# Adaptive max pooling in one dimension: which engine's DMA queue carries the loads and stores

## The chip, the core and the metric

The kernel runs on one core of one Trainium2 chip. The time is device microseconds of one execution; three executions of the kernel before took 335.21, 335.26 and 334.77 us, so the median is 335.21 us. A separate execution was taken with the hardware profiler; its span, from the first to the last instruction, is 333.1 us.

Five engines have instruction streams: PE (TensorE), DVE (VectorE), ACT (ScalarE), POOL (GpSimd) and SP (SyncE). In this kernel only DVE computes. SP and ACT issue DMA transfers. "SPq" and "ACTq" in the profile are the instruction sequencers of SyncE and ScalarE, "q1" and "q10" the DMA queues that the two fill. 16 DMA engines move the bytes of both queues.

## The reference

```
x = randn(32, 256, 4096), float32
output_size = 256
for i in range(output_size):
    start = int(i * length / output_size)
    end = int((i + 1) * length / output_size)
    result[:, :, i] = np.max(x[:, :, start:end], axis=-1)
```

4096 is 256 times 16, so every output is the maximum of its own 16 neighbouring inputs. 134.2 MB are read and 8.4 MB written.

## The kernel before

The input is seen as one long list of windows of W = 16 values, the output as the list of their maxima. There are 2,097,152 windows, or 16,384 for each of the 128 partitions. A "column" is one window in all 128 partitions. A load brings n columns; VectorE reduces them by `reduce_max` over the innermost 16 values (the helper `pooled`, line 56); the maxima of all but the last load stay in SBUF in the tile `kept`.

The 16,384 columns are cut into two groups. Group A has ten loads: FIRST = 128 columns (1,024 KB), eight loads of CHUNK = 1024 columns (8,192 KB each), and one of 1020 columns (8,160 KB). Group B has six loads of 1024 columns and a last one of 900 columns (7,200 KB). Within a group, one partition's windows lie next to each other in memory, so that one partition's share of a load is one contiguous run (64 KB for a load of 1024 columns), and the maxima of a whole group can be stored with one contiguous run for each partition.

The loads go into one tile, `ring`, of 2352 columns. The short first load goes to columns 1024 to 1151 (line 87). The 16 other loads (line 96) alternate between the lower and the upper half, and each half is shifted by GAP = 152 columns every second time. A load may overwrite its place in the ring once VectorE has read what lay there. Because of the shift, the next load into a half needs only the larger part of the chunk before it to be reduced: each chunk is reduced in two instructions, the part that the next load needs first (872 columns), the rest (152 columns) second. So the load with number n + 2 waits for the larger reduction of chunk n, and no longer.

In this text the short first load is called the first load, the 16 others are load 0 to load 15. Load 0 and load 1 wait for nothing; load 2 waits for VectorE's larger reduction of load 0, and also for the landings of the first load and of load 0.

VectorE's instructions run in order: first the first load's reduction (128 columns), then two for each of the loads 0 to 14, then one for load 15, whose 900 maxima are written back into the ring (`last_kept`).

There are three stores: the last store (line 114, 450 KB: the 900 maxima of load 15), and two large ones from `kept` (line 117): store 1 with group A's maxima (4,670 KB) and store 2 with the rest of group B (3,072 KB). `tc.no_sync_barrier()` stands between line 114 and line 117 in the program text. Since each engine runs its own stream, in order, the stores that one engine issues start behind the loads that the same engine issues. In the kernel before, SyncE's stream is: first load, loads 0 to 15, store 1, store 2, then the waits at the end of the program for every transfer (line 148). ScalarE's stream has a single transfer, the last store.

Each waiting transfer waits on its engine's sequencer: an instruction that waits holds up all that is behind it in the same stream.

Of the kernel before, what the change touches and what calls it, by code (L numbers as in the profile page):

```python
# [1 line left out]

# [4 lines left out]


@with_exitstack
def kernel(  # L10
    ctx: ExitStack,
    tc: tile.TileContext,
    x: bass.AP,
    output_size: bass.AP,
    out: bass.AP,
):

    nc = tc.nc
    P = nc.NUM_PARTITIONS
    fp32 = mybir.dt.float32

    B, C, L = x.shape
    O = int(output_size)  # L30
    assert L % O == 0, (L, O)
    W = L // O
    total = B * C * O // P
    assert B * C * O % P == 0

    CHUNK = 1024
    GAP = 152
    FIRST = 128
    LOADS_A, LOADS_B = 9, 6

    LESS = 4
    group_a = [FIRST] + [CHUNK] * (LOADS_A - 1) + [CHUNK - LESS]
    last = total - sum(group_a) - LOADS_B * CHUNK
    group_b = [CHUNK] * LOADS_B + [last]
    assert 0 < last and last * (W + 1) <= CHUNK * W

    pool = ctx.enter_context(tc.tile_pool(name="pool", bufs=1))
    ring = pool.tile([P, 2 * (CHUNK + GAP) * W], fp32, tag="ring", name="ring")
    kept = pool.tile([P, total - last], fp32, tag="kept", name="kept")

    xw = x.flatten_outer_dims().rearrange("r (o w) -> (r o) w", w=W)
    ow = out.flatten_outer_dims().rearrange("r o -> (r o)")

    def pooled(dst, at, n):

        nc.vector.reduce_max(  # L56
            out=dst,
            in_=ring[:, at * W : (at + n) * W].rearrange("p (n w) -> p n w", w=W),
            axis=mybir.AxisListType.X,
        )  # L60

    taken = 0

    def group(n):

        nonlocal taken
        span = slice(taken * P, (taken + n) * P)
        taken += n
        return (
            xw[span].rearrange("(p n) w -> p (n w)", p=P),  # L70
            ow[span].rearrange("(p n) -> p n", p=P),
        )

    stores = []
    n_loads = 0
    base = 0
    for g, loads in enumerate((group_a, group_b)):
        xg, og = group(sum(loads))
        a = sum(loads) if g == 0 else 0
        for n in loads:  # L80
            if g == 0:
                a -= n
            xn = xg[:, a * W : (a + n) * W]
            dst = kept[:, base + a : base + a + n] if n != last else None
            if n == FIRST:

                nc.sync.dma_start(  # L87
                    out=ring[:, CHUNK * W : (CHUNK + n) * W], in_=xn
                )
                pooled(dst, CHUNK, n)  # L90
            else:

                low = n_loads % 2 * (CHUNK + GAP)
                moved = n_loads // 2 % 2
                at = low + moved * GAP
                nc.sync.dma_start(out=ring[:, at * W : (at + n) * W], in_=xn)
                if n != last:
                    cut = CHUNK - GAP if moved else GAP
                    parts = [(0, cut), (cut, n)]
                    for u, v in parts if moved else parts[::-1]:  # L100
                        pooled(dst[:, u:v], at + u, v - u)
                else:
                    end = (at + CHUNK) * W
                    last_kept = ring[:, end - n : end]
                    pooled(last_kept, at, n)
                n_loads += 1
            if g:
                a += n
        full = a - last if g else sum(loads)
        stores.append((og[:, 0:full], kept[:, base : base + full]))  # L110
        base += full
    assert taken == total

    nc.scalar.dma_start(out=og[:, full : full + last], in_=last_kept)
    tc.no_sync_barrier()
    for dst, src in stores:
        nc.sync.dma_start(out=dst, in_=src)


# [1 line left out]
_INS = ['x', 'output_size']  # L121
_OUTS = [((32, 256, 256), 'float32')]

_NUMBERS = {'output_size': 256}


# [26 lines left out]
```

## Time and profile before

| What | us |
|---|---|
| Median of 3 runs | 335.21 |
| Span of the profiled execution | 333.1 |
| VectorE busy (32 instructions) | 276.5 |
| Reduction of 872 columns, mean of 14 | 14.69 |
| Reduction of 152 columns, mean of 15 | 2.68 |
| Reduction of the last 900 columns | 15.14 |
| Reduction of the first 128 columns | 2.29 |
| From one chunk's first reduction to the next one's | 19.35 |
| VectorE idle before each chunk | 2.07 |

The profile gives busy time for engines, the times at which DMA transfers were issued, and the times at which they landed, that is, when their semaphore had its full count. "SPq <- DVE" in a table of waits means that SyncE's sequencer stood at an instruction until VectorE's work released it. The DMA share of a stretch of time is the mean share in which the 16 DMA engines were busy; the rate in GB/s counts all bytes that they moved.

### The profile page before, as it was taken

To read this page: it belongs to the slowest core of one execution; us is meant where nothing else is said; L and a number is where in the kernel's file an instruction comes from. 1 tells how busy PE (TensorE), PEld (TensorE's weight loads), DVE (VectorE), ACT (ScalarE), POOL (GpSimd) and SP (SyncE) were. 2 spreads that over 40 slices of the span, in tenths; PEclk is the share of its full clock that TensorE was granted. 3 is DMA by queue.
4 is the path that set the end of the run, shared out by engine and by line. 5 is a ranking of instruction groups with operands and counts; after the bars stand their busy time and mean duration, and the time that the engine had idled before them with its cause. 6 is when DMAs were issued, how large, how long until landed. Compare 5 with 4: busy or idle time off the path is not lost.

```text
span 333.1 us, 113 instructions
## 1 busy us (share of the span) xinstructions
DVE 276.5 (83%) x32; POOL 0.2 (0%) x4
## 2 busy tenths in 40 slices
DVE  2009979797997979799797979979797998979993
POOL 0000000000000000000000000000000000000000
DMA  9898989899898989899898989899898989899997
GB/s 378 378 504 378 504 378 504 378 449 433 378 504 378 504 378 504 378 441 441 384 494 377 504 378 504 378 456 425 386 496 378 504 378 504 378 458 443 393 395 330
DMA packets 2880, 142.61 MB, mean 428 GB/s; under 512 B 320, under 2 KB 320, under 8 KB 448
## 3 DMA queue, kind: packets, MB, share of 16 engines
q1 hardware_dynamic: 2736, 142.15, 98.8%
q10 hardware_dynamic: 144, 0.46, 0.3%
HBM read 134.22 MB, written 8.39 MB: 428 GB/s over the span
## 4 chain that ended last, share of the span: by engine, by line
DMA 57%; DVE 36%; DVEq 5%; issue 0%; SPq 0%
DMA ring<-in_x_dram 57%; DVE kept L56 36%; DVEq L148 5%; SPq L87 0%
## 5 line engine op out<-in xcount | busy, mean ns | idle before, releaser
L56 DVE TENSOR_REDUCE kept<-ring 128x152 f32<-128x2432 f32 (+3 forms) x31 | 261.4, 8473 | 51.5 <-DMA ring<-in_x_dram 51.5
L56 DVE TENSOR_REDUCE ring<-ring 128x900 f32<-128x14400 f32 x1 | 15.1, 15143 | 0.0
L134 POOL MEMSET const-bfloat16-1.0<- 128x1 bf16 x1 | 0.1, 103 | 0.0
L134 POOL MEMSET const-uint8-127<- 128x1 uint8 x1 | 0.1, 102 | 0.0
L134 POOL MEMSET const-float32-0.0<- 128x1 f32 x1 | 0.1, 100 | 0.2 <-issue 0.2
L134 POOL MEMSET const-float32-1.0<- 128x1 f32 x1 | 0.1, 99 | 0.0
## 6 DMA issues: line engine op xcount, KB each, us to landing
ring<-in_x_dram SPq DMA_DIRECT2D x1, 8160.0 KB, 23.9
ring<-in_x_dram SPq DMA_DIRECT2D x1, 7200.0 KB, 21.7
out_dram<-kept SPq DMA_DIRECT2D x1, 4670.0 KB, 32.4
out_dram<-kept SPq DMA_DIRECT2D x1, 3072.0 KB, 18.2
ring<-in_x_dram SPq DMA_DIRECT2D x1, 1024.0 KB, 4.7
out_dram<-ring ACTq DMA_DIRECT2D x1, 450.0 KB, 4.2
ring<-in_x_dram SPq DMA_DIRECT2D x14, 24.0
```

The lines of the kernel that those rows point to most:

```text
L56: nc.vector.reduce_max(out=dst, in_=ring[:, at * W : (at + n) * W].rearrange("p (n w) -> p n w", w=W), axis=mybir.AxisListType.X,)
L134: nc = _bacc.Bacc("TRN2", target_bir_lowering=False, num_devices=1)
L148: with _tile.TileContext(nc) as tc:
```

## The change

Three words in the program change. The 16 loads of line 96 and the two large stores of line 117 are issued from ScalarE instead of SyncE; the last store of line 114 is issued from SyncE instead of ScalarE. The first load stays on SyncE.

```
-                nc.sync.dma_start(out=ring[:, at * W : (at + n) * W], in_=xn)
+                nc.scalar.dma_start(out=ring[:, at * W : (at + n) * W], in_=xn)
...
-    nc.scalar.dma_start(out=og[:, full : full + last], in_=last_kept)
+    nc.sync.dma_start(out=og[:, full : full + last], in_=last_kept)
     tc.no_sync_barrier()
     for dst, src in stores:
-        nc.sync.dma_start(out=dst, in_=src)
+        nc.scalar.dma_start(out=dst, in_=src)
```

ScalarE's stream is then: loads 0 to 15, store 1, store 2, each with the waits that it had on SyncE. SyncE's stream is: first load, last store, and the waits at the end of the program. The streams of VectorE, GpSimd and TensorE hold the same instructions in the same order. The first load and load 0, which had followed each other on one queue, are on two queues.

## The prediction

> **What bounds the kernel now.** I read the DMA line of the page and a table of stretches first, because 83% busy on VectorE leaves open who waits for whom.
>
> ```profile
> span 333.1 us, 113 instructions
> DVE 276.5 (83%) x32; POOL 0.2 (0%) x4
> ...
> q1 hardware_dynamic: 2736, 142.15, 98.8%
> q10 hardware_dynamic: 144, 0.46, 0.3%
> ```
>
> ```profile
> core 0: us, DVE busy (x) POOL busy (x), PEclk, DMA share, GB/s
> 0.00:1.70 1.70, 0.00 (x0) 0.20 (x4) 1.00 0.00 0
> 1.70:312.60 310.90, 261.11 (x31) 0.00 (x0) 1.00 1.00 434
> 312.60:331.80 19.20, 15.36 (x2) 0.00 (x0) 1.00 0.95 406
> 331.80:333.10 1.30, 0.00 (x0) 0.00 (x0) 1.00 0.00 0
> ```
>
> The two queues' packets fill 99.1% of 16 engines' span. From 1.7 us to the last load's landing the engines are busy all the time, at 434 GB/s; only 1.7 us at the start and 1.3 us at the end hold no packets, and the last 19 us run a little under the rate. So the bytes set the time: 142.61 MB / 434 GB/s = 328.6 us of 333.1. A change of queue can win or lose only at the start, at the end, or where it lets the engines run dry.
>
> Next, how far the engines are from running dry: SyncE's waits, and the order of time around load 2.
>
> ```profile
> SPq L96 <- DVE kept L56: 205.5, 14, 14.7
> SPq L96 <- DMA ring<-in_x_dram: 78.4, 14, 22.7
> SPq L117 <- DVE kept L56: 21.1, 1, 21.1
> ```
>
> ```profile
> 24.78 17.28 DVE L56 TENSOR_REDUCE kept<-ring 128x872 f32<-128x13952 f32 x2 [17.05 <-DMA ring<-in_x_dram]
> 39.49 0.33 SPq L96 DMA_DIRECT2D ring<-in_x_dram  x1
> 44.13 14.69 DVE L56 TENSOR_REDUCE kept<-ring 128x872 f32<-128x13952 f32 x1 [2.07 <-DMA ring<-in_x_dram]
> ```
>
> Fourteen loads are issued the moment VectorE ends an 872-column reduction. Load 2 goes out at 39.49, while load 1 lands at 44.13: the engines have 4.64 us of work left. VectorE idles 2.07 us before each chunk, so a delay of VectorE shrinks by 2.07 us with every chunk.
>
> The issue table gives the latency and the end:
>
> ```profile
> out_dram<-kept SPq DMA_DIRECT2D x1, 4670.0 KB, 32.4
> out_dram<-kept SPq DMA_DIRECT2D x1, 3072.0 KB, 18.2
> ring<-in_x_dram SPq DMA_DIRECT2D x1, 1024.0 KB, 4.7
> out_dram<-ring ACTq DMA_DIRECT2D x1, 450.0 KB, 4.2
> ```
>
> On SyncE the first load, issued at 0.73, lands 4.7 us later; 1.049 MB at 434 GB/s are 2.4, so the lead from issue to steady flow is 2.3 us. On ScalarE the only row is the last store: 4.2 − 0.461 MB / 434 GB/s = 4.2 − 1.1 = 3.1 us, part of which is time behind store 2. I take 2.3 for ScalarE too, the row of the same kind of transfer on idle engines, and keep 3.1 as the upper bound and 2.3 as the lower, since nothing in the trace suggests a shorter one.
>
> **The change part by part.**
>
> *Sixteen loads to ScalarE.* An issue took 0.33 to 0.43 us on SyncE (median 0.33 of 16) and 0.37 on ScalarE: sixteen by +0.04 are 0.6 us of sequencer time. Fourteen lie inside the 4.64 us of work left; with a lead of 2.3 us 2.3 are spare, with 3.1 still 1.5. On the path: 0. Without that cover each issue would cost 0.04 us. The wait list of each load is the same (VectorE and earlier landings), and nothing else runs on ScalarE, so what queues behind a waiting load is again only the next load and the stores.
>
> *Store 1 and store 2 to ScalarE.* They follow load 15 in one stream, as before: store 1 is issued at 291.37 and flows behind the last load (landed 312.64); store 2, which waits 21.1 us for VectorE, goes out at 312.93 and flows behind store 1 (landed 291.37 + 32.4 = 323.8). It has 10.9 us of cover against 2.3 to 3.1. Sum: 0. With no cover the 2.3 to 3.1 would show in full.
>
> *The last store to SyncE.* SyncE's stream holds only the first load ahead of it and the final waits behind it; those waits end with the landings anyway. VectorE ends at 327.96, the issue follows at 327.99. Store 2 lands at 312.93 + 18.2 = 331.1, the last store at 332.2, 1.1 us later, which is just its bytes. So its lead lies beside store 2: with 2.3 us it is ready at 330.3, 0.8 before store 2 is through. Without that cover 2.3 us would show. An issue of 0.33 to 0.43 instead of 0.37 is −0.04 to +0.06 inside those 0.8 us: 0.
>
> *The start.* Load 0 was issued second on SyncE, at 1.16; now ScalarE issues it at once. Released at 0.649 (SyncE) and 0.653 (ScalarE) in the trace, the two begin within 0.01 us of each other, so load 0 and load 1 reach the engines together with the first load. In all, the bytes are the same, so the flow ends at the same time if it begins at the same time. What can change is when it begins (below), and which load comes first. If an engine serves load 0 first, the first load lands not at 5.4 but as late as both loads' bytes, 24.76. VectorE's order is fixed, so it starts with the 128 columns then: 24.78 + 2.29 + 14.69 = 41.76, load 2 goes out at 41.78 instead of 39.49. 44.13 − 41.78 = 2.35 are left against a lead of 2.3: still nothing lost, by 0.05 us. VectorE's 152 columns end at 44.44, 0.3 late for load 1, gone in the next 2.07 of idle time. With the lead of 3.1 it costs 0.8. So this part is 0 to +0.8, and I take 0.
>
> The sum is 0: span 333.1. Outside the span lie 335.2 − 333.1 = 2.1 us, which I keep: 335.2 us, the median of the runs shown (334.77 to 335.26).
>
> **A rule to weigh here.** In the trace each transfer has 144 packets (2736 are 19 transfers, 144 one), nine for each engine. On every engine the last store's packets begin only after store 2's last one, at 330.2 and later, though it was issued at 327.99. Either a begun transfer is finished before another queue gets the engine, or a queue keeps the engine until it is empty; store 2 was the last on its queue, so the trace can't tell. The Trainium skill ("DMA: Bandwidth & Descriptors", section "Queues, rings and completion order") says that an engine takes turns between the queues that have work and changes over after a whole packet of, typically, 9 to 17 descriptors. By that rule the first load waits for load 0 at most and the sum stays 335.2 to 336.0; by the harsher reading of the row it is the third rival's 354.5.
>
> **The rivals.**
>
> *A faster start.* Load 0's issue moves from 1.16 to 0.73, 0.43 us earlier, and two queues are filled at once. First load and load 0 together are 9.44 MB, 21.7 us at 434 GB/s, and landed at 24.76: in effect the flow began at 3.0. The first packet is at 1.75, and a landing comes 0.4 after its packets, so 3.0 − 1.75 − 0.4 = 0.9 us is the most to be had. For it: the first packets took 0.3 to 1.1 us where later ones of their size took 0.31. Against it: no packet can come before the first issue at 0.73, which stays. 334.8 by the issue alone, 334.3 at most.
>
> *Load 2 comes late.* The first load falls behind load 0, and ScalarE's lead is over 2.35 us: then the engines run dry at 43 to 44 us, once. From 2.35 on each microsecond of lead costs one; at 3.1 it is 0.8: 336.0. For it: the dead heat at the start. Against it: the 3.1 contains time behind store 2.
>
> *The first load falls behind load 0 and load 1.* If a queue keeps the engine until it is empty, and ScalarE's is first on even one engine, the first load lands at 44.13. VectorE, which needs it first, then ends load 0's larger part at 44.15 + 2.29 + 14.69 = 61.13; load 2 flows from 61.13 + 2.3 = 63.4 instead of 44.1. That is 19.3 us of empty engines, which nothing later gives back: 354.5. For it: the row above allows it. Against it: SyncE is released first, and it needs both conditions; half for the first and a quarter for the second are 0.12.
>
> That the change does nothing at all is the forecast's own neighbour and gives the same 335.2.
>
> **How the numbers follow.** A difference under 0.2% (0.67 us) can't be told from none here. Forecast, no part on the path: 0.56, of which 0.48 within 0.67 us, 0.04 faster and 0.04 slower by what the runs scatter. Faster start: 0.15, of which 0.08 over 0.67 us. Load 2 late: 0.17, of which 0.10 over 0.67. Behind both loads: 0.12, all slower. Faster 0.04 + 0.08 = 0.12; slower 0.04 + 0.10 + 0.12 = 0.26; same 0.62. Predicted time 335.2. The range goes from 334.3, the faster start's end, to 336.0, load 2 late at the upper lead; the 354.5 and some scatter stay outside.
>
> **What would show it.** Right: the DMA rate stays 434 GB/s from 1.7 us to the last load's landing, the span is 333.1 within 0.7, and VectorE idles 2.07 us before each chunk from load 2 on. First load behind load 0: VectorE's first reduction starts at 20 to 25 us instead of 5.4. Load 2 late: a hole in the DMA share near 43 us. Behind both loads: VectorE idle until 44. Faster start: load 0 lands before 24.7 with all else shifted alike. Wrong in the whole: a DMA rate other than 434 GB/s on ScalarE's queue, which no row of a large load there can exclude.

## The result and the profile after

The changed kernel took 337.62 us in the median of six executions (335.52, 337.45, 337.62, 337.62, 337.66, 337.66), the kernel before 335.09 us beside it. The ratio is 1.0065, with a 95% interval of 1.0052 to 1.0078: it is slower, and outside the range of 334.3 to 336.0 us. The executions form two groups, one at 335.5 and five at 337.5 to 337.7; the profile on record for the changed kernel is of the execution at 335.52 us.

From its page, the span, the queues and the issues (KB, us from issue to landing):

```profile
span 333.7 us, 113 instructions
...
q10 hardware_dynamic: 2592, 141.10, 97.8%
q1 hardware_dynamic: 288, 1.51, 1.3%
...
out_dram<-kept ACTq DMA_DIRECT2D x1, 4670.0 KB, 32.4
out_dram<-kept ACTq DMA_DIRECT2D x1, 3072.0 KB, 18.1
ring<-in_x_dram SPq DMA_DIRECT2D x1, 1024.0 KB, 22.3
out_dram<-ring SPq DMA_DIRECT2D x1, 450.0 KB, 4.2
```

The bytes have changed queues, and the stores land as fast as before (32.4, 18.2 and 4.2 us then). One row is different: the first load takes 22.3 us to land, where it took 4.7. The order of time shows what hangs on it:

```profile
0.72 39.79 ACTq L96 DMA_DIRECT2D ring<-in_x_dram  x3
0.72 0.37 SPq L87 DMA_DIRECT2D ring<-in_x_dram  x1
23.04 19.70 DVE L56 TENSOR_REDUCE kept<-ring 128x128 f32<-128x2048 f32 x3 [23.04 <-DMA ring<-in_x_dram]
44.82 14.69 DVE L56 TENSOR_REDUCE kept<-ring 128x872 f32<-128x13952 f32 x1 [2.08 <-DMA ring<-in_x_dram]
```

VectorE's first reduction starts at 23.04 instead of 5.4, and load 1 is there at 44.82 instead of 44.13, 0.7 late. That is this execution's whole loss. A later profile of the same kernel (the last experiment below) was of an execution at 337.48 us, and its chain of waits, start and length of each piece, shows the rest:

```profile
span 335.7 us, 113 instructions
```

```profile
0.73 24.72 DMA ring<-in_x_dram
25.45 0.02 issue
25.47 16.89 DVE kept L56 x2
42.36 0.02 issue
42.39 23.55 DMA ring<-in_x_dram
65.94 0.02 issue
65.96 14.70 DVE kept L56
```

Now the first load lands at 25.45. VectorE needs 16.89 us for it and for load 0's larger part, load 2 goes out at 42.39 instead of 39.49, and lands at 65.94 instead of 63.45: 2.5 us late. Everything after that runs at the old pace, some 2.5 us later.

The single packets show how the two loads share the engines. Their rows, put together from the trace's packet records (us; for each load the range over the 16 engines; the records do not name the engine, so packets that follow one another without a gap are taken as one engine's):

```
                        before       changed,     changed,
                                     335.52 us    337.48 us
load 0, last ends       23.96-24.40  23.99-25.08  24.04-25.07
load 1, last ends       43.28-43.73  43.31-44.40  43.37-44.40
load 2, first starts    43.28-43.73  43.31-44.40  43.70-45.39
load 2, last ends       62.60-63.08  62.76-63.72  63.73-65.58
last packet of all      331.72       332.37       334.34
```

On each engine a packet of the first load (8 KB) and one of load 0 (64 KB, 2.42 us) take turns, one by one. Eight such turns put the end of the first load beside the end of load 0. In the execution at 335.52 us two packets of the first load came ahead of load 0's first on every engine, so its ninth packet, the 4 bytes that count the landing, went in front of load 0's eighth. In the one at 337.48 us only one came ahead, and that ninth packet had to wait behind load 0's eighth: 2.42 us, within 0.01 the difference between 23.04 and 25.47. The loss of 2.5 us then has two parts in the table, read on the slowest engine: 0.67 at the start (25.07 against 24.40) and 1.83 where load 2 arrives (65.58 − 63.08 − 0.67). Ten of the 16 engines ran dry, for up to 2.0 us. The engine that ended load 2 last was through with load 1 at 43.55, got load 2's first packet at 45.36 and took 3.30 us for it instead of 2.42.

### The profile page after: what moved, and what is told of

It is laid out like the page before. It is cut to its first block, busy times and chain, and to the rows that moved or that the text cites. A ratio compares the mean times of both kernels' runs of the same rounds, so it can differ in the third digit from the quotient of the medians.

```text
span 333.7 us, 113 instructions
## 1 busy us (share of the span) xinstructions
DVE 276.5 (83%) x32; POOL 0.2 (0%) x4
## 4 chain that ended last, share of the span: by engine, by line
DMA 58%; DVE 36%; DVEq 5%; issue 0%
DMA ring<-in_x_dram 58%; DVE kept L56 36%; DVEq L148 5%
## 6 DMA issues: line engine op xcount, KB each, us to landing
out_dram<-kept ACTq DMA_DIRECT2D x1, 4670.0 KB, 32.4
ring<-in_x_dram SPq DMA_DIRECT2D x1, 1024.0 KB, 22.3
```

## The experiments

The executions of the kernel before that ran beside these had medians of 334.93 to 335.03 us. "Order theory" and "queue theory" are explained in the first expectation below.

**The changed kernel again.** No edit.

> The changed kernel again. Of its six executions one took 335.5 us (the profiled one) and five 337.5 to 337.7. Order theory: ScalarE's load 0 and SyncE's first load start in a dead heat; where load 0's packets come first on the engines, the first load's last packets fall behind packets of load 1 (2.4 us each), it lands at 26 to 27 us, VectorE comes late to load 0, load 2 goes out at about 44 instead of 40 us, and the engines run dry for about 2 us. It expects two groups of times again, near 335.5 and near 337.6, and nothing between. Queue theory: ScalarE's queue is itself slower, by a slower start of some engines or a lower rate; it expects times that spread evenly from 335.5 upward, and load 2 issued near 40 us in every profile.

Measured: 335.72 once, the profiled one, and 337.08 to 337.83 five times; ratio 1.0065 (1.0049 to 1.0081). The profile has the first load at 23.26 and load 2 at 40.40. Two groups and nothing between, as the order theory has it, but the profile shows only the group that loses little.

**VectorE's order.** The first load goes to a place that load 2 does not need, and is reduced behind load 0's larger part:

```
-                    out=ring[:, CHUNK * W : (CHUNK + n) * W], in_=xn
+                    out=ring[:, 2200 * W : (2200 + n) * W], in_=xn
...
-                pooled(dst, CHUNK, n)
+                late = (dst, 2200, n)
...
                         pooled(dst[:, u:v], at + u, v - u)
+                        if late is not None:
+                            tc.no_sync_barrier()
+                            pooled(*late)
+                            late = None
```

> The changed kernel, but the first load goes to columns 2200 to 2327 (which load 3 and not load 2 overwrites) and VectorE reduces it after load 0's 872 columns, so nothing on the way to load 2 waits for the first load. The two loads still race at the start. Order theory: all executions at 335.0 to 335.8 us, whichever load comes first, VectorE's first reduction at 24.4 to 25.5 and load 2 issued 14.7 us later, at 39 to 40.3. Queue theory: the loss does not depend on VectorE's order, so most executions stay at 337 to 338 us.

Measured: 335.45 to 335.72 us in eleven executions, ratio 1.0016 (1.0007 to 1.0025). The chain of waits:

```profile
0.72 25.07 DMA ring<-in_x_dram
25.80 0.02 issue
25.82 14.70 DVE kept L56
40.52 0.02 issue
40.54 23.80 DMA ring<-in_x_dram
```

In the profiled execution only one packet of the first load came ahead on every engine, as in the one at 337.48 us, and it still took 335.71 us. The upper group is gone, so its 1.9 us pass through VectorE's wait for the first load. What remains, 0.6 us, is the start itself: load 0 is there at 25.82 instead of 24.78. VectorE's order has no part in that.

**SyncE held back.** One line ahead of the first load:

```
+                nc.vector.memset(ring[:, CHUNK * W : CHUNK * W + 64], 0.0)
```

> The changed kernel, but the first load waits for a memset of 64 values per partition in its place by VectorE, so that SyncE issues it 0.1 to 0.4 us after ScalarE's load 0. Order theory: load 0's packets come first on all engines; the first load lands at 24.4 to 27 us, load 2 goes out at 41.5 to 44.2, and all executions are in the upper group, 337 to 338.5 us, the profiled one too, with a hole in the DMA work near 44 us. Queue theory: the small delay of a load that is not the bound changes nothing: the same mixture as the changed kernel, load 2 near 40 us.

Measured: 336.75 to 337.78 us in five executions, ratio 1.0068 (1.0056 to 1.0080). SyncE issued 0.23 us behind ScalarE, and load 0's packets came first on all engines:

```profile
25.44 16.89 DVE kept L56 x2
42.33 0.02 issue
42.35 23.57 DMA ring<-in_x_dram
```

A delay of 0.23 us of 1 MB makes every execution, the profiled one too, one of the upper group.

**ScalarE held back.** Two lines after the first load's issue:

```
+                nc.vector.memset(ring[:, 0:64], 0.0)
+                nc.vector.memset(ring[:, (CHUNK + GAP) * W : (CHUNK + GAP) * W + 64], 0.0)
```

> The changed kernel, but load 0 and load 1 wait for two memsets of 64 values per partition in their places by VectorE, so that ScalarE issues load 0 0.1 to 0.5 us after SyncE's first load. Order theory: the first load's packets come first on all engines, it lands by 23 us at the latest, load 2 goes out by 40.3, and all executions are at 335.0 to 335.9 us. Queue theory: most executions stay at 337 to 338 us.

Measured: 334.78 to 335.43 us in eleven executions, ratio 0.9999 (0.9991 to 1.0008). ScalarE issued load 0 at 0.95:

```profile
10.41 2.29 DVE L56 TENSOR_REDUCE kept<-ring 128x128 f32<-128x2048 f32 x1 [9.41 <-DMA ring<-in_x_dram]
24.92 17.28 DVE L56 TENSOR_REDUCE kept<-ring 128x872 f32<-128x13952 f32 x2 [12.23 <-DMA ring<-in_x_dram]
44.27 14.69 DVE L56 TENSOR_REDUCE kept<-ring 128x872 f32<-128x13952 f32 x1 [2.07 <-DMA ring<-in_x_dram]
```

The first load is there at 10.4, and the whole loss is gone, the 0.6 us of the start too.

**All on ScalarE.** The first load as well:

```
-                nc.sync.dma_start(
+                nc.scalar.dma_start(
                     out=ring[:, CHUNK * W : (CHUNK + n) * W], in_=xn
```

> The changed kernel with the first load on ScalarE too, so that first load and load 0 follow each other on one queue, as in the kernel before, and ScalarE's queue carries all loads and the large stores. Order theory: no race, so the first load lands near 5.4 us, load 2 goes out near 39.5, and all executions are at 334.8 to 335.4 us: ScalarE's queue itself costs nothing. If ScalarE's queue or its issue cost something of their own, the time stays above 335.6 us.

Measured: 335.01 us, ratio 1.0001 (0.9993 to 1.0010), VectorE's first reduction at 5.34, load 2 at 39.39. ScalarE's queue, its issues and the exchanged stores cost nothing that can be measured.

**Both edits.** SyncE held back as above, and VectorE's order changed as above.

> Both edits together: SyncE's first load is held back by the small memset, so that load 0 is first on every engine, and VectorE reduces the first load after load 0's 872 columns, from columns 2200 on. Order theory: the first load lands at 24.5 to 26 us as with the held-back SyncE, but nobody needs it then; load 2 goes out at 39.5 to 40.5 and all executions are at 334.8 to 335.8 us, some 2 us under the kernel with SyncE held back alone. If the order on the engines costs time other than through VectorE's wait, it stays at 337 to 338 us.

Measured: 335.08 to 335.47 us in eleven executions, ratio 1.0006 (0.9998 to 1.0015). Load 0 first on the engines costs some 2 us when VectorE waits for the first load, and next to nothing when it doesn't.

**VectorE late, the queues as before.** The kernel before, with k columns of load 0 reduced once more:

```
+                    if n_loads == 0:
+                        pooled(dst[:, 0:128], at + cut, 128)
                     for u, v in parts if moved else parts[::-1]:
```

> The kernel before, all queues as before; VectorE reduces 128 columns of load 0 one time more ahead of the 872, with the result written where a later reduction writes again. That is 2.29 us, so load 2 goes out at 41.8 instead of 39.5 us. The prediction's price for this lateness was nothing to 0.8 us (335.0 to 335.9). The held-back SyncE run showed load 2's first packets 1.4 to 3.3 us after its issue, engine by engine, while engines run dry from 43.3 us on: by that it is 0.5 to 1.8 us (335.5 to 336.8).

Measured: 335.01 us, ratio 1.0001 (0.9992 to 1.0010), with load 2 at 41.71 us:

```profile
41.71 22.03 DMA ring<-in_x_dram
```

The prediction's own point, that 2.3 us of lateness are just hidden, holds on SyncE; the price of 0.5 to 1.8 us that I read from the run with SyncE held back does not.

With 152 columns:

> The same with 152 columns instead of 128: 2.68 us, load 2 at 42.15 us, close to the 42.35 of the run with SyncE held back. Order theory with VectorE's wait as its only path: 336.5 to 337.6 us with no change of queue at all, and 0.3 to 0.5 us over the run with 128 columns, since past the point where engines run dry each microsecond costs one. If the loss needs two queues, it stays at 335.0 to 335.3 us.

Measured: eight executions at 335.10 to 335.44 us, four at 338.01 to 339.03; ratio 1.0040 (1.0015 to 1.0066). The profiled one, of 335.10 us, issued load 2 at 41.97, and no engine waited for it by more than 0.2 us:

```profile
41.97 21.74 DMA ring<-in_x_dram
```

The four have no profile. If they are the ones in which engines ran dry, the edge lies within some tenths of a microsecond of 42, and who falls over it loses 3 us or more at once, with only one queue in use; that is not shown.

With 224 and 320 columns, the result written to `kept` where it is replaced later:

> The kernel before, with 224 columns of load 0 reduced one time more ahead of the 872 (the result goes to a place that is written later): about 3.9 us, load 2 goes out at about 43.3 us. With 2.29 us nothing was lost; with 2.68 us the executions split into 335.1 to 335.4 and 338.0 to 339.0. Jump theory: once the engines are dry the restart itself costs 2.5 to 3.5 us (engines start again at different times), and each microsecond of lateness adds about one: all executions at 338.5 to 340. Slope theory: the loss is only the lateness past about 41.9 us: 336.2 to 336.8.

> The same with 320 columns: about 5.5 us, load 2 at about 44.9 us. Jump theory: 1.6 us over the run with 224 columns, 340 to 341.6. Slope theory: 337.8 to 338.4.

Measured: 336.59 us (336.42 to 336.81; ratio 1.0049, 1.0035 to 1.0062) and 338.38 us (338.17 to 338.67; ratio 1.0104, 1.0089 to 1.0120). The first one's chain:

```profile
24.85 18.49 DVE kept L56 x2
43.34 0.02 issue
43.36 21.96 DMA ring<-in_x_dram
65.32 0.02 issue
```

And of the second one's:

```profile
44.96 21.81 DMA ring<-in_x_dram
```

Here the slope theory is right: load 2 goes out at 43.36 and 44.96, 1.60 apart, and the times are 1.79 apart. By that slope the changed kernel's issue at 42.39 would cost 0.5 us; it cost 1.83. So near the edge there is a price that the lateness does not explain. The packets show a difference: with 224 columns, where all engines had ended load 1 by 43.77, load 2 starts within 0.88 us on all of them (44.32 to 45.20) and ends within 0.65 (64.35 to 65.00); in the changed kernel's execution at 337.48 us, where some engines still worked on load 1, it starts over 1.69 us (43.70 to 45.39) and ends over 1.85. The load is there only when its slowest engine is done.

**The mirror.** First load from ScalarE, the rest from SyncE:

```
-                nc.sync.dma_start(
+                nc.scalar.dma_start(
                     out=ring[:, CHUNK * W : (CHUNK + n) * W], in_=xn
```

(an edit of the kernel before)

> The mirror of the change: the first load from ScalarE, load 0 to 15 and the large stores from SyncE, the last store from ScalarE. The race at the start is the same, with the engines exchanged. If the loss comes from two loads racing on two queues, it is there again in part or in all executions, 335.5 or 337 to 338 us. If ScalarE is ahead of SyncE in the race whatever it carries, then the first load is now first on the engines: it lands by 23 us, and all executions are at 334.9 to 335.8.

Measured: 336.55 to 337.83 us in five executions, ratio 1.0070 (1.0057 to 1.0083).

```profile
25.67 16.89 DVE kept L56 x2
42.56 0.02 issue
42.57 22.68 DMA ring<-in_x_dram
```

Here SyncE's load 0 was first on every engine. The loss belongs to the race of two queues, not to ScalarE.

**The changed kernel once more.** No edit, for another profile.

> The changed kernel once more, for its profile: both profiles so far are of executions at 335.5 and 335.7 us, with the first load at 23.0 and 23.3 us. If the race falls differently between executions, a profile can show the other outcome: the first load at 25 us or later, load 2 at 42 us or later and some 337.5 us. Otherwise a third one near 335.6 us.

Measured: 337.48 us; its profile is shown with the result. It is the outcome that the order theory had put together from the other runs, with one correction: the packets that push the first load back are load 0's own, not load 1's.

None of these kernels beats the kernel before by more than can be measured; the one with ScalarE held back and the one with all loads on ScalarE equal it.

## Why the prediction was wrong, point by point

- *The bytes set the time, at 434 GB/s.* Right, on ScalarE's queue too: all of the loss lies before load 2 has landed.
- *Sixteen loads to ScalarE, 0.* Right: with all loads there, 1.0001 (0.9993 to 1.0010).
- *The stores, 0.* Right: same landings, and the same run.
- *The start, "0 to +0.8, and I take 0".* This is the step that failed, and with it the predicted time. Its mechanism was right: the dead heat, the first load landing with load 0, VectorE's fixed order, load 2 late. Two terms in it were mis-sized. The first is the start of the flow, taken as unchanged: on the slowest engine the shared start took 0.67 us longer, so the first load landed at 25.45, not 24.76, and load 2 went out at 42.39, not 41.78. The second is the lead of 2.3 us, at most 3.1. The spare time was as forecast: load 1 landed at 44.81 by the trace's landing records, 2.42 us after load 2's issue (the forecast had 2.35). But load 2 took 23.55 us to land, and its bytes at 434 GB/s are 19.3 of them, so by the prediction's own reckoning the lead was 4.2. That is 1.8 us over the spare time, the 1.83 of the table; with the 0.67 it makes 2.5. The same reckoning gives 2.6 and 2.5 with 224 and 320 columns (21.96 and 21.81 us to land), so 2.3 was nearly right for engines that are all empty, and wrong where some were and some were not. The landing of load 1 was also the wrong moment to count to: the first engine had run out of load 1 at 43.37, 0.98 us after the issue, and load 2's first packets came 1.3 to 3.0 us after it. In the profiled run with 152 columns the first engine ran out 1.46 us after the issue (43.43 against 41.97), and nothing was lost. A result that rests on 0.05 us of spare time should not have been the forecast with 0.56.
- *Rival "load 2 comes late", 336.0.* This is what happened, in place and in kind; it was priced at 0.8 and given 0.17.
- *Rival "behind load 0 and load 1", 354.5.* It did not come: even with load 0 first on every engine the first load was there at 25.4. Both readings of the last store's packets (a transfer is finished first, or a queue keeps the engine) are wrong for these loads: the queues alternate packet by packet. The row needs neither reading: the prediction's own lead puts the last store's first packets at 330.3, and they came at 330.2. The trace of before had the first load and load 0 on one queue and could not show it.
- *Rival "a faster start", 334.3 to 334.8.* The shared start is slower, by 0.6 us in the run with VectorE's order changed. With load 0 issued at 0.95 instead of 1.16, and the first load ahead, nothing was gained.

What stays open: what decides whether one or two packets of the first load come ahead. ScalarE issued 0.005 us ahead of SyncE in all three profiles. Three executions of the changed kernel were seen packet by packet, two of the lower and one of the upper group; the ten others, all in the upper group, were seen by their time only. Both executions of the lower group are profiled ones, and no run shows whether the profiler shifts the race. Why a restart near the edge is so uneven was not tried either, and the executions of 338 to 339 us with 152 columns have no profile.

## What to carry to other kernels

Here two transfers on one queue kept their order, and on two queues they shared each engine packet by packet. Both loads had eight data packets on each engine, so the small one finished about when the large one did. So before a small load that others wait for is put on a queue of its own beside a large one, look at what waits for it: here VectorE's fixed order turned 20 us of lateness, harmless in itself, into a late issue of load 2 at 42 us. Where a ring's spare time and the lead of a transfer agree to a tenth of a microsecond, count the case as lost. Count the spare time to the moment at which the first engine runs out (0.98 us was too little here), and price the loss by the slowest engine, not by the mean.

## What the runs showed of the hardware that I had not expected

- Two queues alternate on an engine after every single packet, even of 8 KB against 64 KB, and the 4 bytes that count a landing wait for their own turn: 2.42 us here. The Trainium skill ("DMA: Bandwidth & Descriptors", section "Queues, rings and completion order") has an engine change over after typically 9 to 17 descriptors. If each packet of the trace is one descriptor, that is about a whole transfer's share of an engine here (nine packets), and these runs do not agree.
- The first packets after a start are slow: 64 KB took 3.0 to 3.2 us on average where load 0 came first on idle engines, and 2.9 to 3.1 us at load 2 after engines had run dry, against 2.42 us in the flow.
- Every engine moved eight of a load's 128 large packets, late or not, so an unevenness lasts: the 1.85 us between the engines at load 2's end were still there at load 3's (83.05 to 84.93).
